# Hybrid decoder layer, its last two token chunks: output projections placed earlier, block sums of the activations made in the up stage, and the sums handed to VectorE

## The chip, the cores and the metric

One core of one Trainium2 chip runs the whole layer. The metric is the device time of one execution in microseconds (us); several executions are taken and their median is compared. Five engines work side by side, each in its own fixed order: TensorE (PE, its weight loads listed apart as PEld), VectorE (DVE), ScalarE (ACT), GpSimd (POOL), and SyncE (SP), which only issues DMAs. ACT issues DMAs as well.

## The reference, cut to what matters

One layer with three groups of heads (mLSTM, RWKV-7, differential attention) on 2048 tokens of width 1024, then an output projection, a feed-forward network (FFN) and a final norm:

```python
def _rms_norm(x, g, eps=NORM_EPS):
    xf = x.astype(jnp.float32)
    y = xf * lax.rsqrt(jnp.mean(jnp.square(xf), axis=-1, keepdims=True) + eps)
    return (y * g.astype(jnp.float32)).astype(x.dtype)
...
        mix = jnp.concatenate([y_m, y_r, y_a], axis=-1).astype(x.dtype)
        x = x + mix @ w_out[l]
        h = _rms_norm(x, norm2_g[l])
        x = x + jnp.square(jax.nn.relu(h @ w_ff_up[l])) @ w_ff_down[l]
    return _rms_norm(x, final_g)
```

The FFN is 1024 to 4096 and back. All of it is float32.

## The kernel before, in words

**Precision.** Every float32 product is three matmuls on a number cut in two (`split`, L174 and L175): ACT copies the high part (`whi`, `uh`, `hh`), VectorE or GpSimd subtracts it to get the low part (`wlo`, `ul`, `hl`), and TensorE adds high by high, high by low and low by high (L182 to L184 in `mm3`, L1219 to L1221 in `Wino.prod`). So each tile of weights costs one ACT and one DVE or POOL instruction before TensorE can use it.

**Stages.** Tokens are four chunks of 512. Projections, mLSTM, RWKV and attention run first; then `Tail` does, chunk by chunk, the output projection (`outproj`, 192 matmuls) and the FFN. Chunks 0 and 1 have a plain FFN (`ffn`), a loop of 16 steps `fb` with 48 up and 48 down matmuls each. Chunks 2 and 3 share one FFN by the Strassen-Winograd scheme (`Wino`): 7 block products instead of 8, at the price of sums of blocks. `first` norms chunk 2 and cuts its 8 tiles; `second` norms chunk 3, forms the sums t1 to t4 and cuts them; `up` makes the hidden layer and stores its activations to DRAM (`act`); `down` loads them again; `final` is the last norm. In all of them p counts the 7 products.

- `up`: 8 steps fb, 7 products p, two halves q of 12 matmuls each. The sums of weight blocks (`factors`, L1284 to L1290) are on VectorE, all low parts on GpSimd. The results are 4 blocks of 16 tiles, so 64 stores.
- `down`: 4 stages st, 7 products of 48 matmuls. VectorE makes sums of the loaded activations (L1368 to L1376, 16 tiles of 128x512 a stage), GpSimd makes the sums of weight blocks (L1284 to L1290, 8 tiles of 128x1024 a stage) and the low parts of the weights (28 a stage); VectorE makes the low parts of the activations (28 a stage). Each product has its own four PSUM banks, and VectorE adds them to an accumulator in SBUF (L1411). In the last stage 28 sums of accumulators on GpSimd (L1408, L1410) and 4 on VectorE (L1413) join the 7 products to the four blocks of the result.

**Placing.** `tile_hybrid_layer` runs chunk 1's FFN loop. It overlaps the attention of chunk 3, whose waits its matmuls fill. At `fb == 12` the attention's pools are closed (`actx.close()`), the pools of the next stage open in their place, and the output projection of chunk 2 starts; a step of it follows at fb 13 and 14; at fb 15 `Wino.first`, at fb 16 the output projection of chunk 3. Then comes `final(1, ...)` (chunk 1's norm and output) and `second`.

**What sets the order.** The order on each engine is fixed when the program is built: a scheduler places the instructions by their dependences and by priority (`high_priority`), with its own estimate of time. Pools bind it: a tile in a newly opened pool can't be written before the last reader of the closed pool. The norm's sum of squares (`nacc`, L155 to L168) has one buffer, so two norms can't overlap.

Of the kernel before, what the change touches and what calls it, by code (L numbers as in the profile page):

```python
# [20 lines left out]
P = 128  # L21
# [1179 lines left out]
class Wino:  # L1201
# [33 lines left out]
    def first(s, x2, hp):  # L1235

        nc = s.tc.nc
        with s.tc.high_priority():
            s.rms(x2)
            s.b11 = s.cut(x2[:4], [s.tl.hl(hp) for _ in range(4)], (nc.vector, nc.gpsimd))  # L1240
            s.b21 = s.cut(x2[4:], [s.tl.hl(hp) for _ in range(4)], (nc.vector, nc.gpsimd))

    def second(s, x2, x3, tp):
# [3 lines left out]
        with s.tc.high_priority():  # L1247
# [3 lines left out]
            for k in range(4):  # L1251
                G.tensor_tensor(b12[k], b22[k], b12[k], ALU.subtract)
                V.tensor_tensor(b11[k], b12[k], b11[k], ALU.add)
                t2 += s.cut(b11[k:k + 1], [tl.hl()], (V,))
            for k in range(4):
                t3 += s.cut(b12[k:k + 1], [tl.hl()], (G, V))
# [3 lines left out]
            for k in range(4):  # L1260
                G.tensor_tensor(b21[k], b21[k], b11[k], ALU.subtract)
                t4 += s.cut(b21[k:k + 1], [tl.hl(tp)], (V,))
# [3 lines left out]
    def factors(s, ring, bufs, a, eng):  # L1266

        nc = s.tc.nc

        def new():  # L1270
            return ring.tile([P, 1024], F32, name="wr", tag="wr", bufs=bufs)

        def ld(x):
            t = new()
            s.e.dq += 1
            load(nc, s.e.dq, t.rearrange("p (k c) -> p k c", k=x.shape[1]), x)
            return t
        a11 = ld(a[0])
        yield a11
        a12 = ld(a[1])  # L1280
        yield a12
        s3, a22 = ld(a[2]), ld(a[3])
        s2 = new()
        eng.tensor_tensor(s3, a11, s3, ALU.subtract)  # L1284
        eng.tensor_tensor(s2, a22, s3, ALU.subtract)
        yield s2
        yield s3
        s1, s4 = s3, s2
        eng.tensor_tensor(s1, s2, a11, ALU.add)
        eng.tensor_tensor(s4, a12, s2, ALU.subtract)  # L1290
        yield s1
        yield a22
        yield s4

    def unit(s, x, eng, shape):
# [3 lines left out]
        h3, l3 = [t.rearrange("p (k c) -> p k c", k=shape) if shape else t for t in (hi, lo)]  # L1299
# [3 lines left out]
    def up(s):  # L1303
        tc, nc, tl, e = s.tc, s.tc.nc, s.tl, s.e
        V, A = nc.vector, nc.scalar
        for fb in range(8):
            f = s.factors(s.wr, 6, [tl.wu[fb + 8 * m][:, 4 * k:4 * k + 4] for m in range(2) for k in range(2)], V)
            ps = [[None] * 3 for _ in range(2)]
            c1, u2, u3 = [[None] * 2 for _ in range(3)]

            def put(m, c, x, r):
                A.activation(r, x, AF.Relu)
                A.activation(r, r, AF.Square)
                nc.sync.dma_start(e.act[c][m], r)
            for p in range(7):
                b = (0, 0, 1, 1, 2, 1, 2)[p]
                new = p in (0, 2, 4)
                with tc.high_priority():
                    w = next(f).rearrange("p (k c) -> p k c", k=4)
                    w = [s.unit(w[:, :, q * P:(q + 1) * P], nc.gpsimd, 4) for q in range(2)]  # L1320
                for q in range(2):
                    if new:
                        ps[q][b] = s.bank(1 + b)
                    o = ps[q][b]
                    for k in range(4):
                        s.prod(o, w[q][0][:, k * P:(k + 1) * P], w[q][1][:, k * P:(k + 1) * P], s.ops[p][k], new and k == 0)
                    m = 2 * fb + q
                    with tc.high_priority():
                        if p == 0:
                            c1[q] = tl.slot(0)  # L1330
                            A.copy(c1[q], o)
                        elif p in (2, 3):
                            t = tl.slot(4)
                            V.tensor_tensor(t, o, c1[q], ALU.add)
                            (u2 if p == 2 else u3)[q] = t
                        else:
                            r = tl.slot(5)
                            if p == 1:
                                put(m, 0, o, r)
                            else:  # L1340
                                V.tensor_tensor(r, o, {4: u3, 5: c1, 6: u2}[p][q], ALU.add)
                                put(m + 16 * (p != 6), p != 5, r, r)

    def down(s, ap, ar, wr2):
        tc, nc, tl, e = s.tc, s.tc.nc, s.tl, s.e
        V, A, G = nc.vector, nc.scalar, nc.gpsimd
        grp = [0, 2, 3, 4, 5]
        acc = [[ap.tile([P, T], F32, name="acc", tag=f"a{p}{q}") if p < 6 else tl.slot(1) for q in range(4)] for p in range(7)]
        with tc.high_priority():
            for p, c, d in ((1, 0, 0), (5, 0, 4), (6, 1, 0)):  # L1350
# [3 lines left out]
        def features(st):  # L1354
            def ld(g, c, m):
                x = [tl.slot(g) for _ in range(4)]
                for k in range(4):
                    load(nc, k, x[k], e.act[c][m + k])
                return x
            g = grp  # L1360
            m = 4 * st
            b11 = ld(g[0], 0, m)
            yield b11
# [266 lines left out]
```

## Time and profile before

| | |
|---|---|
| median of 3 runs | 3099.58 us (3095.73 to 3113.41) |
| profiled execution | 3101.93 us, its span 3100.2 us |
| mean granted clock of TensorE | 0.964 of 2.4 GHz |
| busy in the span | PE 2893.9 us (93%), DVE 1911.5 (62%), POOL 1391.0 (45%), ACT 1299.1 (42%) |
| chunk 2's and 3's `up` | 2394 to 2693 us |
| their `down` | 2693 to 3070 us |
| after the last matmul of a product | 3069.66 to 3100.2 us |

Busy time is summed by engine; a busy PE is not a PE at its peak. The granted clock is given as a share of 2.4 GHz, so 0.50 is 1.2 GHz. In a window's row "x" counts instructions, and "released by" (the arrow) names the instruction that ended a wait. The 1.7 us between the span and the profiled time lie around the program.

### The profile page before, as it was taken

To read this page: it belongs to the slowest core of one execution; us is meant where nothing else is said; L and a number is where in the kernel's file an instruction comes from. 1 tells how busy PE (TensorE), PEld (TensorE's weight loads), DVE (VectorE), ACT (ScalarE), POOL (GpSimd) and SP (SyncE) were. 2 spreads that over 40 slices of the span, in tenths; PEclk is the share of its full clock that TensorE was granted. 3 is DMA by queue.
4 is the path that set the end of the run, shared out by engine and by line. 5 is a ranking of instruction groups with operands and counts; after the bars stand their busy time and mean duration, and the time that the engine had idled before them with its cause. 6 is when DMAs were issued, how large, how long until landed. Compare 5 with 4: busy or idle time off the path is not lost. (4 is left out here: it accounts for less than half of the span.)

```text
span 3100.2 us, 47371 instructions
## 1 busy us (share of the span) xinstructions
PE 2893.9 (93%) x16848; PEld 2365.7 (76%) x16848; DVE 1911.5 (62%) x4141; ACT 1299.1 (42%) x2577; POOL 1391.0 (45%) x1213
## 2 busy tenths in 40 slices
PE   8999999999999789999999999999984999899995
PEld 7877887778878677888888788887863888777773
DVE  6587879677872557555556855554347333379995
ACT  5333334232322445444544554444333555443342
POOL 4354444333332124333433333333445444487787
PEclk9999999999999899999999999999996999999997
DMA  8445333643634553443446334424441333533201
GB/s 304 127 148 193 85 93 81 222 113 88 202 108 126 152 144 110 127 110 88 120 116 177 112 96 114 111 82 138 144 149 43 121 109 110 207 119 102 87 24 54
DMA packets 303270, 383.97 MB, mean 124 GB/s; under 512 B 100885, under 2 KB 162614, under 8 KB 302010
## 3 DMA queue, kind: packets, MB, share of 16 engines
q1 hardware_dynamic: 218634, 264.93, 28.5%
q10 hardware_dynamic: 84400, 116.02, 12.6%
q8 instruction: 133, 2.18, 0.3%
q14 instruction: 103, 0.84, 0.1%
HBM read 285.66 MB, written 95.18 MB: 123 GB/s over the span
## 5 line engine op out<-in xcount | busy, mean ns | idle before, releaser
L175 POOL TENSOR_TENSOR wlo<-wraw,whi 128x512 fp32r<-128x512 f32 (+2 forms) x432 | 593.7, 1387 | 859.6 <-ACT whi L174 608.2
L175 POOL TENSOR_TENSOR wlo<-wr,whi 128x512 fp32r<-128x512 f32 x224 | 325.0, 1461 | 222.2 <-ACT whi L174 194.3
L174 ACT ACTIVATE whi<-wraw 128x512 fp32r<-128x512 f32 (+2 forms) x432 | 267.1, 625 | 325.8 <-PE pd L183 103.2
L183 PE MATMUL pd<-hl,whi 128*128 128x512 f32 x768 | 304.5, 397 | 6.9 <-DVE hl L175 6.9
L182 PE MATMUL pd<-hh,whi 128*128 128x512 f32 x768 | 302.3, 398 | 5.8 <-ACT hh L174 5.3
L184 PE MATMUL pd<-hh,wlo 128*128 128x512 f32 x768 | 301.2, 396 | 0.1
L1174 DVE TENSOR_TENSOR x<-py,x 128x512 f32<-128x512 f32 x256 | 174.8, 688 | 197.2 <-PE py L184 196.1
L1030 DVE TENSOR_SCALAR_CACHE_REDUCE E<-pS 128x512 f32<-128x512 f32 (+4 forms) x320 | 185.6, 607 | 147.9 <-PE pS L1027 88.5
L174 ACT ACTIVATE whi<-wr 128x512 fp32r<-128x512 f32 x224 | 139.7, 629 | 290.9 <-PE pd L1220 121.6
L182 PE MATMUL pd<-hhi,whi 128*128 128x512 f32 x544 | 222.9, 413 | 7.7 <-ACT hhi L279 6.7
L184 PE MATMUL pd<-hhi,wlo 128*128 128x512 f32 x544 | 222.2, 411 | 0.6 <-POOL wlo L175 0.6
L183 PE MATMUL pd<-hlo,whi 128*128 128x512 f32 x544 | 221.9, 410 | 0.7 <-DVE hlo L280 0.3
L182 PE MATMUL py<-ah,whi 128*128 128x512 f32 x512 | 207.0, 405 | 1.2 <-DVE x L1174 0.6
L183 PE MATMUL py<-al,whi 128*128 128x512 f32 x512 | 203.2, 397 | 0.4 <-DVE al L175 0.4
L184 PE MATMUL py<-ah,wlo 128*128 128x512 f32 x512 | 201.6, 397 | 0.0
L1037 ACT ACTIVATE E<-E,nm 128x128 f32<-128x128 f32 (+15 forms) x128 | 153.7, 1201 | 91.1 <-DVE nm L1033 73.9
L182 PE MATMUL pd<-whi,hhi 128*128 128x256 f32 (+1 forms) x640 | 187.1, 293 | 1.2 <-ACT gates L372 0.9
L183 PE MATMUL pd<-wlo,hhi 128*128 128x256 f32 (+1 forms) x640 | 186.9, 292 | 0.0
L175 DVE TENSOR_TENSOR ul<-x,uh 128x512 fp32r<-128x512 f32 x112 | 155.8, 1404 | 49.1 <-ACT uh L174 49.1
L184 PE MATMUL pd<-whi,hlo 128*128 128x256 f32 (+1 forms) x640 | 185.7, 290 | 0.0
L183 PEld LDWEIGHTS pd<-hl,whi 128*128 128x128 f32 x768 | 145.7, 190 | 37.6 <-DVE hl L175 7.3
L182 PEld LDWEIGHTS pd<-hh,whi 128*128 128x128 f32 x768 | 145.3, 190 | 37.2 <-issue 5.6
(447 smaller groups left out, 7302.9 us busy)
## 6 DMA issues: line engine op xcount, KB each, us to landing
wraw<-in_wu ACTq DMA_DIRECT2D x64, 256.0 KB, 3.1
wraw<-in_wu SPq DMA_DIRECT2D x64, 256.0 KB, 3.2
wraw<-in_wd ACTq DMA_DIRECT2D x64, 256.0 KB, 3.3
wraw<-in_wd SPq DMA_DIRECT2D x64, 256.0 KB, 3.0
act<-x SPq DMA_DIRECT2D x64, 256.0 KB, 2.0
wraw<-in_wi ACTq DMA_DIRECT2D x48, 256.0 KB, 3.5
wraw<-in_wi SPq DMA_DIRECT2D x48, 256.0 KB, 3.6
feat<-hhi SPq DMA_DIRECT2D x4, 2048.0 KB, 9.7
```

The lines of the kernel that those rows point to most:

```text
L174: nc.scalar.activation(hi, src, AF.Copy)
L175: lo_eng.tensor_tensor(lo, src, hi.bitcast(F32), ALU.subtract)
L182: nc.tensor.matmul(out, sh, mh, start=(i == 0), stop=False)
L183: nc.tensor.matmul(out, sh, ml, start=False, stop=False)
L184: nc.tensor.matmul(out, sl, mh, start=False, stop=(i == n - 1))
L1030: V.tensor_scalar(E[:, k0:k0 + w], s_[:, :w], 0.125, None, ALU.mult, ALU.max, accum_out=mb[:, j:j + 1])
L1037: A.activation(E[:, :n], E[:, :n], AF.Exp, bias=nm, accum_out=l)
L1174: nc.vector.tensor_tensor(x2[d], ps, x2[d], ALU.add)
```

## The change

1. The attention's pools are closed at `fb == 8` instead of 12. The output projection of chunk 2 runs at fb 8 to 12, `Wino.first` at fb 12 instead of 15, the output projection of chunk 3 at fb 12 to 15 instead of after the loop.
2. `up` takes its products in another order and half q after half (12 matmuls a product). Low parts are on GpSimd for 3 of 7 products and on VectorE for 4; the sums of weight blocks are made per half on VectorE. The sums of activation blocks are made here, four a half on VectorE, and all 7 blocks are stored: 112 stores instead of 64. Three PSUM banks are each used for two or three products of a half, and what the first left is read before the next adds to it.
3. `down` loads 7 finished blocks (112 loads) and makes no sums of them. The sums of weight blocks move to VectorE; the low parts of weights go half to GpSimd, half to VectorE. PSUM banks of one product are kept and added to by a later one (`NEW`, `BANK`), so 24 sums of accumulators are left in the last stage, 20 on VectorE and 4 on GpSimd. (Of `final(2, ...)` 2 tiles instead of 8 are on GpSimd.)

```diff
+    NEW = (0, 1, 4)
+    BANK = (0, 1, 0, 1, 2, 1, 2)
...
-                G.tensor_tensor(b12[k], b22[k], b12[k], ALU.subtract)
+                V.tensor_tensor(b12[k], b22[k], b12[k], ALU.subtract)
...
-        s.ops = [s.b11, s.b21, t2, t3, t1, t4, c22]
+        s.ops = [s.b11, t2, s.b21, t3, t1, t4, c22]
...
+            for q in range(2):
+                f = s.factors([t.rearrange("p (k c) -> p k c", k=4)[:, :, q * P:(q + 1) * P] for t in w])
...
+                        h, l = s.unit(next(f), nc.gpsimd if p in (0, 3, 5) else V, 4)
+                    if p in s.NEW:
+                        ps[s.BANK[p]] = s.bank(1 + s.BANK[p])
...
+                    V.tensor_tensor(b12, b22, b12, ALU.subtract)
+                    put(3, b12)
+                    V.tensor_tensor(b11, b12, b11, ALU.add)
+                    put(1, b11)
+                    V.tensor_tensor(t1, b22, b11, ALU.subtract)
+                    put(4, t1)
+                    V.tensor_tensor(b21, b21, b11, ALU.subtract)
+                    put(5, b21)
...
-                        w = s.unit(ws[k // 2][:, k % 2 * T:k % 2 * T + T], G, 0)
+                        w = s.unit(ws[k // 2][:, k % 2 * T:k % 2 * T + T], V if k % 2 else G)
...
-                            for i in {1: (0,), 2: (0,), 3: (2,), 5: (3,), 6: (2, 4)}.get(p, ()):
-                                G.tensor_tensor(a, a, acc[i][q], ALU.add)
...
+                            for y, z, eng in {0: ((x22[q], a[0], G), (a[5], a[0], V)), 1: ((a[1], a[0], V), (a[6], a[1], V)),
+                                              3: ((x22[q], a[3], V),), 4: ((x22[q], a[4], V),)}.get(p, ()):
+                                eng.tensor_tensor(y, y, z, ALU.add)
...
-        if fb == 12:
+        if fb == 8:
             actx.close()
...
+        if 8 < fb < 12:
+            next(op)
+        if fb == 12:
+            list(op)
+            wn = Wino(tl, wr, pq)
+            wn.first(x2)
+            op = tl.outproj(3, tl.load(3, hp2), x3, (4, 5), pq[1], e.x2d[1])
```

**In the program's order, TensorE, end of chunk 3's attention.** L1051 are transposes and L1056 products of the last head, L1068 the transposes of its output; `pd<-hh,whi` and `py<-ah,whi` are matmuls of chunk 1's FFN. Before, they stand around the transposes:

```order
L182 MATMUL py<-ah,whi 128x512
L183 MATMUL py<-al,whi 128x512
L184 MATMUL py<-ah,wlo 128x512
L182 MATMUL py<-ah,whi 128x512
L1068 MATMUL pT<-ident,osb 128x128 x2
L183 MATMUL py<-al,whi 128x512
L1068 MATMUL pT<-ident,osb 128x128 x2
L184 MATMUL py<-ah,wlo 128x512
L183 MATMUL pd<-hl,whi 128x512
L184 MATMUL pd<-hh,wlo 128x512
```

In the changed kernel the same place reads as follows; here the first `pd` after the transposes is the output projection of chunk 2.

```order
L1056 MATMUL pO<-Vt,PT 128x128 x4
L1051 MATMUL pT<-ident,E 128x128 x4
L1056 MATMUL pO<-Vt,PT 128x128 x4
L1051 MATMUL pT<-ident,E 128x128 x4
L1056 MATMUL pO<-Vt,PT 128x128 x4
L1051 MATMUL pT<-ident,E 128x128 x4
L1056 MATMUL pO<-Vt,PT 128x128 x4
L1068 MATMUL pT<-ident,osb 128x128 x4
L182 MATMUL pd<-hh,whi 128x512 x2
L183 MATMUL pd<-hl,whi 128x512
L184 MATMUL pd<-hh,wlo 128x512
```

FFN matmuls no longer stand between the last head's steps, and the output projection follows it directly.

**VectorE, a product of `down`.** L175 makes low parts, L1411 adds PSUM to an accumulator. Before, the sums of activations (L1373, L1376) stand between them:

```order
L1411 TENSOR_TENSOR acc<-pd,acc 128x512 x2
L175 TENSOR_TENSOR ul<-x,uh 128x512
L1373 TENSOR_TENSOR x<-x 128x512
L1376 TENSOR_TENSOR x<-x 128x512
L175 TENSOR_TENSOR ul<-x,uh 128x512
L1373 TENSOR_TENSOR x<-x 128x512
L1376 TENSOR_TENSOR x<-x 128x512
```

In the changed kernel the low parts of weights (`wlo`) and the sums of weight blocks (128x1024) stand there:

```order
L1411 TENSOR_TENSOR acc<-pd,acc 128x512 x2
L175 TENSOR_TENSOR wlo<-wr,whi 128x512
L175 TENSOR_TENSOR ul<-x,uh 128x512 x2
L1286 TENSOR_TENSOR wr<-wr 128x1024
L175 TENSOR_TENSOR wlo<-wr,whi 128x512
L175 TENSOR_TENSOR ul<-x,uh 128x512 x2
L175 TENSOR_TENSOR wlo<-wr,whi 128x512
L175 TENSOR_TENSOR ul<-x,uh 128x512
L1287 TENSOR_TENSOR wr<-wr 128x1024
```

VectorE has lost the sums of activations and gained two `wlo` a product and the wide sums.

**GpSimd, `down`.** Before, wide sums (L1284 to L1290) stand among the low parts of weights:

```order
L1289 TENSOR_TENSOR wr<-wr 128x1024
L175 TENSOR_TENSOR wlo<-wr,whi 128x512
L1284 TENSOR_TENSOR wr<-wr 128x1024
L1290 TENSOR_TENSOR wr<-wr 128x1024
L175 TENSOR_TENSOR wlo<-wr,whi 128x512 x5
L1285 TENSOR_TENSOR wr<-wr 128x1024
L1284 TENSOR_TENSOR wr<-wr 128x1024
L175 TENSOR_TENSOR wlo<-wr,whi 128x512 x5
```

In the changed kernel this is all that GpSimd has from the cuts of `second` to the end:

```order
L175 TENSOR_TENSOR hl<-x,hh 128x512 x5
L175 TENSOR_TENSOR x<-x 128x512
L175 TENSOR_TENSOR wlo<-wr,whi 128x512 x92
L1416 TENSOR_TENSOR x<-x,acc 128x512 x4
L175 TENSOR_TENSOR wlo<-wr,whi 128x512 x9
L134 TENSOR_TENSOR nsm<-nsm,nhalf 128x4
L1192 TENSOR_TENSOR acc<-acc,nacc 128x512 x2
L134 TENSOR_TENSOR nsm<-nsm,nhalf 128x4
L1192 TENSOR_TENSOR x<-x,nacc 128x512 x3
```

One kind of work is left there, with half the number of tiles per product of `down`.

## Rows read from the trace of the kernel before

**Rows 1.** Page, part 1: busy time and share of the span.

```profile
PE 2893.9 (93%) x16848; PEld 2365.7 (76%) x16848; DVE 1911.5 (62%) x4141; ACT 1299.1 (42%) x2577; POOL 1391.0 (45%) x1213
```

**Rows 2.** Windows: length, busy time (instructions) per engine, granted clock, DMA share, GB/s.

```profile
1025.00:1125.00 100.00, 72.89 (x340) 54.51 (x339) 59.97 (x232) 48.28 (x136) 17.14 (x14) 0.81 0.58 162
2035.00:2146.00 111.00, 111.00 (x580) 94.02 (x579) 50.66 (x97) 47.17 (x84) 40.60 (x30) 1.00 0.26 80
2146.00:2249.00 103.00, 97.67 (x412) 78.48 (x411) 38.66 (x47) 40.67 (x70) 47.12 (x36) 0.97 0.53 166
2249.00:2331.00 82.00, 71.95 (x292) 57.28 (x291) 40.70 (x54) 29.42 (x50) 39.04 (x29) 0.92 0.46 138
2331.00:2394.00 63.00, 21.85 (x70) 14.54 (x69) 47.44 (x51) 18.25 (x33) 34.72 (x22) 0.64 0.14 50
2394.00:2693.00 299.00, 299.00 (x1296) 245.22 (x1297) 104.77 (x124) 151.22 (x252) 149.54 (x109) 0.99 0.34 118
2400.00:2675.00 275.00, 275.00 (x1203) 225.68 (x1202) 91.21 (x106) 140.45 (x233) 137.47 (x101) 1.00 0.33 113
2693.00:3070.00 377.00, 336.95 (x1355) 261.70 (x1353) 311.58 (x282) 146.94 (x261) 298.53 (x172) 0.95 0.28 88
2712.00:3070.00 358.00, 327.09 (x1322) 254.16 (x1320) 305.97 (x273) 139.51 (x248) 294.48 (x169) 0.96 0.24 73
```

**Rows 3.** Waits of PE, 2100 to 3101: total, times, longest.

```profile
PE nps L162 <- DVE nacc L159: 30.8, 4, 15.2
PE pd L1220 <- DVE ul L175: 18.9, 12, 4.0
PE pd L1219 <- ACT whi L174: 9.1, 1, 9.1
PE pd L1221 <- POOL wlo L175: 5.7, 3, 3.8
```

**Rows 4.** Groups by form in 2712 to 3070: busy, mean ns, idle before.

```profile
L175 POOL TENSOR_TENSOR wlo<-wr,whi 128x512 fp32r<-128x512 f32 x107 | 165.1, 1558 | 51.3 <-ACT whi L174 46.9 <-PE pd L1220 4.4
L175 DVE TENSOR_TENSOR ul<-x,uh 128x512 fp32r<-128x512 f32 x105 | 149.0, 1431 | 41.0 <-ACT uh L174 41.0
L1411 DVE TENSOR_TENSOR acc<-pd,acc 128x512 f32<-128x512 f32 x60 | 39.5, 679 | 5.6 <-PE pd L1221 4.3 <-POOL acc L1408 1.2
L1376 DVE TENSOR_TENSOR x<-x 128x512 f32<-128x512 f32 x16 | 30.8, 1923 | 0.4
L1290 POOL TENSOR_TENSOR wr<-wr 128x1024 f32<-128x1024 f32 x8 | 22.6, 2828 | 0.0
```

**Rows 5.** Timeline: store of the last head, then what waits (ACT, PE).

```profile
2147.33 0.33 SPq L1071 DMA_DIRECT2D mixT<-ot  x1
2154.44 0.63 ACT L174 ACTIVATE hh<-traw 128x512 fp32r<-128x512 f32 x1 [6.08 <-DMA mixT<-ot]
2155.17 1.19 PE L182 MATMUL pd<-hh,whi 128*128 128x512 f32 x2 [4.93 <-ACT hh L174]
```

**Rows 6.** Timeline: one half block of attention (DVE, ACT, DVE).

```profile
2099.56 0.69 DVE L1030 TENSOR_SCALAR_CACHE_REDUCE E<-pS 128x512 f32<-128x512 f32 x1 [0.21 <-PE pS L1027]
2101.10 2.01 ACT L1037 ACTIVATE E<-E,nm 128x2048 f32<-128x2048 f32 x1 [1.41 <-DVE nm L1033]
2104.43 2.34 DVE L1045 SCALAR_TENSOR_TENSOR E<-E,rat 128x2048 f32<-128x2048 f32 x1
2110.97 0.35 DVE L1057 TENSOR_SCALAR osb<-pO,orl 128x128 f32<-128x128 f32 x1 [0.44 <-PE pO L1056]
```

**Rows 7.** Timeline: chunk 1's final norm, then `down`'s first weights.

```profile
2337.24 1.26 POOL L175 TENSOR_TENSOR wlo<-wr,whi 128x512 fp32r<-128x512 f32 x1 [1.17 <-ACT whi L174]
2338.53 1.23 DVE L1289 TENSOR_TENSOR wr<-wr 128x1024 f32<-128x1024 f32 x1 [0.88 <-POOL wlo L175]
2695.32 0.69 DVE L175 TENSOR_TENSOR ul<-x,uh 128x512 fp32r<-128x512 f32 x1 [1.29 <-ACT uh L174]
2700.35 0.58 SPq L42 DMA_DIRECT2D wr<-in_wd  x1
2707.92 0.79 PE L1219 MATMUL pd<-uh,whi 128*128 128x512 f32 x1 [9.14 <-ACT whi L174]
```

**Rows 8.** Timeline: the end.

```profile
3066.65 9.86 POOL L1192 TENSOR_TENSOR acc<-acc,nacc 128x512 f32<-128x512 f32 x8 [4.79 <-ACT nacc L168]
3076.54 0.63 ACT L155 ACTIVATE nacc<-x 128x512 f32<-128x512 f32 x1 [9.96 <-POOL acc L1192]
```

More of the change, by code (lines that the diff above doesn't have):

```diff
@@ L1233, in cut, with first @@
         return pairs
-    def first(s, x2, hp):
+    def first(s, x2):
         nc = s.tc.nc
@@ L1239, in first, with second @@
             s.rms(x2)
-            s.b11 = s.cut(x2[:4], [s.tl.hl(hp) for _ in range(4)], (nc.vector, nc.gpsimd))
-            s.b21 = s.cut(x2[4:], [s.tl.hl(hp) for _ in range(4)], (nc.vector, nc.gpsimd))
-    def second(s, x2, x3, tp):
+            s.b11 = s.cut(x2[:4], [s.tl.hl() for _ in range(4)], (nc.vector, nc.gpsimd))
+            s.b21 = s.cut(x2[4:], [s.tl.hl() for _ in range(4)], (nc.vector, nc.gpsimd))
+    def second(s, x2, x3, hp, tp):
         nc, tl = s.tc.nc, s.tl
@@ L1306, in up @@
         for fb in range(8):
[L1307 to L1324, printed above, removed]
+            with tc.high_priority():
+                w = s.blocks(s.wr, 6, [tl.wu[fb + 8 * m][:, 4 * k:4 * k + 4] for m in range(2) for k in range(2)])
@@ L1379, in down, with four @@
+        def four(src, again=True):
+            g = grp.pop(0)
+            if again:
+                grp.append(g)
+            x = [tl.slot(g) for _ in range(4)]
+            for k in range(4):
+                load(nc, k, x[k], src[k])
+            return x
         for st in range(4):
             last = st == 3
-            x = features(st)
-            f = [s.factors(r, n, [tl.wd[2 * st + i + 8 * k][:, :, T * m:T * m + T] for m in range(2) for k in range(2)], G)
-                 for i, (r, n) in enumerate(((s.wr, 6), (wr2, 5)))]
+            with tc.high_priority():
+                f = [s.factors(s.blocks(r, b, [tl.wd[2 * st + i + 8 * k][:, :, T * m:T * m + T] for m in range(2) for k in range(2)]))
+                     for i, (r, b) in enumerate(((s.wr, 6), (wr2, 5)))]
+            ps = {}
@@ L1396, in down @@
                     if last and p == 0:
-                        x22 = [tl.slot(grp[4]) for _ in range(4)]
-                        for q in range(4):
-                            load(nc, q, x22[q], e.x2d[1][4 + q])
+                        x22 = four(e.x2d[1][4:], False)
                     for q in range(4):
-                        a = acc[p][q]
-                        if st == 0 and p in (0, 2, 3, 4):
-                            A.copy(a, ps[q])
+                        a = [t[q] for t in acc]
@@ L1441, in tile_hybrid_layer @@
     e.av = [scr(f"av{h}", [HALF, 512]) for h in range(2)]
[L1442 removed]
+    e.act = [[scr(f"act{c}_{m}", [P, T]) for m in range(FF // P // 2)] for c in range(7)]
     e.x2d = [[scr(f"x2d{c}_{d}", [P, T]) for d in range(KT)] for c in range(2)]
@@ L1547, in tile_hybrid_layer @@
             list(op)
-            wn = Wino(tl, wr, pq)
-            wn.first(x2, hp2)
-            m3 = tl.load(3)
-        if fb == 16:
-            for _ in tl.outproj(3, m3, x3, (4, 5), None, e.x2d[1]):
-                pass
     tl.final(1, x1, (2, 5))
```

144 lines of the change are left out of this document (68 added, 76 removed).

## Prediction

> **What bounds the kernel now.** First the busy shares: TensorE works 93% of the span [rows 1]. Unless its matmuls become fewer, and they don't, a change can only win back the other 7% and stretches at the lower clock. So the second view is the windows, to find where TensorE is not full. While attention and chunk 1's FFN run together (2035 to 2146) and in `up` it is full; 1203 matmuls in 275 us are 0.2286 us each, which I take as its pace [rows 2]. It loses time in three places. From 2146 to 2331 the 704 matmul records would need 161 us and take 185: 24 lost. From 2331 to 2394, around chunk 1's final norm and the norm of chunk 3, it is busy 21.85 of 63 us, at a mean clock of 0.64. And `down`, 2693 to 3070, holds 4 x 7 x 48 = 1344 matmuls, which need 307 us and take 377: 70 lost, the largest sum, and the one this change is about. Third, what PE waits for [rows 3]: the norms' sums (L162, 30.8 us), then low parts from VectorE (18.9) and GpSimd (5.7), and once 9.1 us for the first weights of `down`. Last, the two engines that make these low parts. In 2712 to 3070 VectorE is busy 306 and GpSimd 294 of 358 us [rows 2], so each looks as if it had room. The groups say otherwise: a 128x512 low part takes VectorE 1431 ns and GpSimd 1558 on the mean, a sum of activations (L1376) VectorE 1923 [rows 4], but 0.69 and 1.26 us where the other is idle [rows 7]; VectorE's additions out of PSUM, in the same stretch, keep to 679 ns [rows 4]. So the two slow each other down only where both inputs of VectorE lie in SBUF. Counted at the undisturbed times, GpSimd has 107 low parts and 28 sums x 1.26 and 30 wide sums x 2.52 (twice 1.26, an estimate), 246 us; VectorE has 105 low parts and 56 sums x 0.69, 111 us. Together 357 of 358 us: taken as one server the pair is full, and TensorE waits for it.
>
> The Trainium skill, page SBUF — State Buffer, section Who interferes with whom, has a rule for that: a VectorE instruction with two inputs in SBUF and a GpSimd instruction that reads SBUF exclude each other for their whole length, and one with a single SBUF input doesn't take part. The 1431, 1558 and 679 ns agree with it. By it, work that only changes sides stays in the same queue, so that of the moved sums only the shorter time on VectorE counts. With neither engine waiting for the other there would be no full server before (246 and 111 of 358 us), and the change would win in `down` only the 3 us of its entry, for some 3114 us in all.
>
> **The change part by part**, each against the profiled execution, 3101.9 us (the median lies 2.3 us lower).
>
> 1. `down`. Removed: 16 sums of activations a stage, and 28 + 4 sums of accumulators in the last one, of which 4 on GpSimd and 20 on VectorE remain. Moved from GpSimd to VectorE: 32 wide sums, at 1.23 us [rows 7] instead of 2.8 [rows 4], and half of the weights' low parts. After it GpSimd has 56 low parts and 4 sums, 60 x 1.26 = 76 us. VectorE has 112 + 56 low parts and 20 sums x 0.69 = 130, and 32 x 1.23 = 39, so 169 with both inputs in SBUF, and 96 additions out of PSUM x 0.68 = 65. The pair needs 245 instead of 357 us where TensorE needs 307. VectorE alone has 234; if every GpSimd instruction held it up, 310. So TensorE sets the pace again but for four things: the last stage, where p = 0 has 6 GpSimd instructions (7.6 us), 10 low parts and sums of VectorE (6.9) and a wide sum or so (1.4), 15.9 against the 11.0 of 48 matmuls, and p = 1 has 13.6: with the norm of chunk 2 some 10 us lost; the entry, 6 us (below); and in-order waits of single products, 8. Loss 24 instead of 70: **46 won**. Bounds: 30, if all of GpSimd's time holds VectorE up and the single waits cost 20; 54, if only the entry and the last stage cost. I take 46 because the pair's load falls by a third and the waits of PE here are of that pair's making [rows 3]. What was hidden stays so: 48 more loads of 256 KB run on DMA engines whose share here is 0.24 [rows 2].
>    The entry: TensorE waits 9.14 us, since the weights for k = 2 and 3 are only issued on SP at 2700.35, behind stores [rows 7]. After it, ACT issues them behind its last square; I price it at 6 (4 to 9).
>
> 2. The output projections. What the order shows decides here: with the pools closed at fb 8, FFN matmuls of later steps no longer stand between the steps of chunk 3's last head. Before, they filled its waits wholly: 111.00 of 111 us [rows 2]. Three and a half blocks of that head are left bare. A block occupies VectorE with 8 maxima of 0.69 or less, the scaling of 2.34 and small ones, some 8.5 us [rows 6]; 3.5 x 8.5 = 30; the last one ends with the exponential (2.0), the scaling (2.3) and 4.2 from there to the last L1057 [rows 6], and some 2 for the head's norm: 41 us, of which the matmuls fill about 25 (an estimate from their number). 16 lost. Then the output projection needs the stored head: from the issue of the store at 2147.33 to the cut at 2154.44 are 7.1 us [rows 5], and with copy and cut 9; before, FFN matmuls covered all but 4.93 of it. Its later tiles arrive at the pace of VectorE's cuts (4), and the clock has to rise again (3, an estimate). 32 lost against 24 before, and in exchange chunk 2's norm and chunk 3's projection run among FFN matmuls, which I price at nothing lost: the FFN of four steps covers them, and without this cover they cost the 20 that lie in those 24 besides the store. **8 lost** (5 won, if only store and cut cost; 25 lost, by A below).
>
> 3. The gap of 63 us between the FFN and `up` stays: `final(1, ...)` still precedes chunk 3's norm, by the one buffer. Off VectorE's path in it go the wide sums between L164 and L144, 2 x 1.23 [rows 7] and one more; on it come 4 subtractions from GpSimd (2.8), and TensorE has 12 matmuls less to fill with (2.7). **0** (8 either way).
>
> 4. `up`. A half is 84 matmuls, 19.2 us. In it VectorE has 4 low parts, 4 sums of weights, 4 of activations and 5 evictions, 17 x 0.69 = 11.7, GpSimd 3 x 1.26 = 3.8: 15.5 of 19.2 even in turn. ACT keeps its work (151 of 299 us [rows 2]). New is the hand-over of banks: four times a half a product adds to a bank that was filled two products earlier, with one product, 12 x 0.2286 = 2.74 us, to read it. An eviction of 0.69 leaves 2 us of room, more than one foreign instruction. **5 lost** over 64 hand-overs (0 to 15). 48 more stores stand on SP; its loads stand behind them, one step ahead.
>
> 5. The end. `final(3)` waits for GpSimd's 8 multiplications, 9.86 us to 3076.5, 6.9 after the last matmul [rows 8]. VectorE takes 6 of them, but behind its last additions: 9 after. **2 lost** (1 to 3).
>
> Sum: 46 - 8 - 0 - 5 - 2 = 31 us won, 3071 from the profiled execution; beside the median I put **3070**.
>
> **Rivals.**
> A. The bare head costs more. In 1025 to 1125, attention with little beside it, TensorE is busy 72.89 of 100 us at a clock of 0.81 [rows 2], so 59 us of work. By that the head's 25 and the projection's first 17 us of work take 71, 29 lost instead of 16, and with half clock on the wait for the store some 49 in all: 25 lost in step 2 and 46 - 25 - 5 - 2 = 14 won, **3088**: no change. For it: the windows in which TensorE idles have the lower clocks, 0.81 here and 0.64 at 2331 [rows 2]. Against it: that stretch also waits for loads at its start.
> B. Slower: the hand-over of banks in `up`. If an eviction stands behind two foreign instructions at the disturbed 1.43 to 1.75 us, it ends 3.7 us after the product or later, 1 us past the 2.74; from 2.74 on every microsecond is TensorE's. 64 x 1.0 = 64 lost in step 4 instead of 5, and 46 - 8 - 64 - 2 = 28 lost: **3130**. For it: VectorE's queue is in order, and sums that wait for ACT's squares stand in it. Against it: GpSimd has 3 instructions in 19.2 us.
> C. VectorE inherits the limit in `down`: if its instructions with two SBUF inputs keep the 1.43 us [rows 4], 188 of them and 32 wide ones at twice the 1.23 are 348 us, and with 65 out of PSUM over 400; with half of that increase, 169 + 90 + 65 = 324, and 45 for entry, last stage and single waits `down` takes 369: 8 won instead of 46, 7 lost in all, **3109**, no change. Against it: the increase is GpSimd's time, which falls from 294 to about 76.
>
> **How the numbers follow.** Forecast 0.66, spread from 3040 (steps 1 to 4 at their better ends, not all) to 3084; A 0.14, C 0.06, B 0.14. The measurement tells about 0.5%, 15 us. Faster 0.66, same 0.20, slower 0.14. The range takes in A and C and leaves out B and a little below: 3040 to 3110.
>
> **What would show it.** Step 1: `down` lasts about 331 us from its first matmul, VectorE's low parts near 0.8 us, GpSimd busy under 110 us in it, waits for `ul` gone. Step 2: windows of TensorE under 20 of 25 us around 2070 to 2130 that weren't there, and the 2146 to 2331 losses gone. Step 4: waits of PE in `up` named after evictions would speak for B. It is wrong if `down` stays over 350 us, or the bare head loses over 40.

## The result, and the profile after

The changed kernel takes 3089.26 us (median of 18 runs, 3078.06 to 3100.93) against 3104.89 (18 runs, 3095.73 to 3118.53) of the kernel before on the same chip: ratio 0.9949, 95% interval 0.9936 to 0.9962, that is 15.8 us less (12 to 20). The forecast was 3070, some 31 us won. The time lies in the stated range, the sign is right, and the size is half of what was forecast, at the edge of the 0.5% that the prediction could tell apart.

The profiled execution of the changed kernel took 3098.3 us, with a span of 3096.6. The two traces can't be laid over each other from the start: the same attention matmul (L1026, the 20th from the last) begins at 2025.2 us before and at 2035.7 after, though the same 12794 matmul records stand ahead of it, all but 8 of them in the same places. In the traces of the experiments this point lies between 2025 and 2049 us, with no relation to what was changed. So only what follows it is compared: 1075.0 us before, 1060.9 after, 14.1 less, which agrees with the medians.

Page, part 1, of the changed kernel, to be read beside [rows 1]; GpSimd has lost 321 us, VectorE gained 36:

```profile
PE 2898.9 (94%) x16848; PEld 2376.1 (77%) x16848; DVE 1947.5 (63%) x4355; ACT 1297.8 (42%) x2571; POOL 1069.5 (35%) x1023
```

Windows of the changed kernel, columns as in [rows 2]: the last head; the wait for its store; the rest of the FFN with both projections; the gap around the norms; `up`; the entry to `down` (two rows); the rest of it; the end.

```profile
2036.00:2098.00 62.00, 48.26 (x265) 39.53 (x263) 25.64 (x70) 23.03 (x40) 8.44 (x6) 0.82 0.12 36
2098.00:2111.00 13.00, 1.20 (x4) 0.70 (x4) 3.35 (x6) 2.01 (x4) 0.00 (x0) 0.50 0.66 222
2111.00:2363.00 252.00, 248.66 (x1060) 201.08 (x1058) 105.22 (x140) 98.96 (x168) 120.87 (x89) 0.98 0.42 130
2363.00:2420.00 57.00, 20.97 (x62) 13.35 (x61) 43.25 (x62) 20.52 (x36) 19.55 (x12) 0.61 0.10 37
2420.00:2714.00 294.00, 293.08 (x1279) 240.12 (x1279) 189.31 (x264) 145.38 (x244) 61.80 (x46) 1.00 0.43 150
2714.00:2750.00 36.00, 14.61 (x52) 11.13 (x51) 9.99 (x16) 8.91 (x16) 0.50 (x1) 0.75 0.97 351
2750.00:3062.00 312.00, 312.00 (x1327) 250.84 (x1326) 251.26 (x314) 135.73 (x240) 89.56 (x60) 0.99 0.37 121
3062.00:3096.00 34.00, 5.58 (x15) 2.71 (x13) 20.92 (x28) 7.92 (x13) 8.53 (x6) 0.56 0.33 123
```

The reader is to see a new hole at 2036 to 2111, a longer one at 2714 to 2750, and a `down` that is full from 2750 to its end, where before it was busy 327 of 358 us [rows 2]. In the entry the DMA engines are busy for 0.97 of the time. Before, the share was 0.28 over the whole of `down` [rows 2], but its entry was as full as now, only shorter:

```profile
2693.00:2712.00 19.00, 9.86 (x35) 7.53 (x34) 5.61 (x9) 7.43 (x13) 4.05 (x4) 0.77 1.02 364
```

What PE waits for in the changed kernel, 2030 to 3100:

```profile
PE nps L162 <- DVE nacc L159: 30.2, 4, 13.6
PE pd L1223 <- ACT whi L174: 15.8, 1, 15.8
PE pd L182 <- ACT hh L174: 11.8, 1, 11.8
PE pd L1223 <- ACT hh L174: 11.4, 1, 11.4
PE nps L145 <- DVE traw L144: 9.8, 4, 2.7
PE pO L1056 <- ACT PT L1053: 9.3, 10, 2.3
PE pd L1223 <- ACT uh L174: 5.5, 1, 5.5
PE py L1223 <- ACT x L1336: 2.3, 1, 2.3
```

The 18.9 us for `ul` and 5.7 for `wlo` of [rows 3] are gone. In their place stand single long waits: 11.8 for the first cut tile of chunk 2's projection, 5.5 and 15.8 at the entry to `down` (before, one of 9.1 [rows 3]). One wait only, of 2.3 us, is put down to an eviction in `up`, ACT's copy (L1336).

The groups in `down`, 2791 to 3062, beside [rows 4]: `ul` has fallen from 1431 to 948 ns, while GpSimd's `wlo` is nearly as slow as it was (1506 against 1558); VectorE's new `wlo` takes 750, its additions out of PSUM 679 as before.

```profile
L175 DVE TENSOR_TENSOR ul<-x,uh 128x512 fp32r<-128x512 f32 x94 | 88.8, 948 | 13.7 <-ACT uh L174 13.7
L175 POOL TENSOR_TENSOR wlo<-wr,whi 128x512 fp32r<-128x512 f32 x46 | 69.3, 1506 | 182.5 <-ACT whi L174 171.6 <-PE pd L1225 6.7 <-DVE x L1416 4.2
L1411 DVE TENSOR_TENSOR acc<-pd,acc 128x512 f32<-128x512 f32 x57 | 37.4, 679 | 8.4 <-PE pd L1225 8.4
L175 DVE TENSOR_TENSOR wlo<-wr,whi 128x512 fp32r<-128x512 f32 x46 | 34.5, 750 | 19.5 <-ACT whi L174 19.5
```

To see where the time went I add up, for each stretch of each trace, the time from the start of one matmul to the start of the next, less 0.2273 us for 512 columns and in proportion for fewer. The rest is TensorE's lost time (idle, or at half clock). The few matmuls of the norms (L145, L162) have prices of their own; in strict proportion the head would be 0.6 higher and the middle 1.8 in every row, and the body 0.4, or 1.8 where it is that of before. "Head" runs from the L1026 named above to the last L1068, "middle" on to the last FFN matmul, "gap" to 15 us after the last norm before `up`, "entry" from up's end over the first 192 matmuls of `down`, "body" over its other 1152. Us:

```
                      head  middle  gap    up   entry  body
before                10.2   25.8  47.4   4.7   13.2   55.5
after                 33.7   24.0  44.1   2.6   28.2    8.5
old placing (e1)      10.2   25.6  41.8   4.4   29.2    8.4
new placing only (e2) 31.4   20.6  48.5   4.5   13.9   54.0
late residuals (e3)   33.7   23.5  44.1   2.6   21.9    8.4
GpSimd sums (e4)      32.8   21.4  44.1   2.6   25.0   17.0
closed at 10 (e5)     26.1   22.3  44.6   2.6   26.6    8.5
halves swapped (e6)   33.7   23.6  44.2   3.9   21.9    8.5
16 more sums (e8)     32.8   21.1  44.1   2.6   21.2   19.2
both of these (e9)    33.7   23.4  44.0   2.7   29.7   53.1
weights ahead (e10)   33.7   23.4  44.0   4.1   20.1    8.4
closed at 12 (e12)    10.2   18.3  44.1   2.6   25.9    8.4
all together (e11)    10.2   18.4  44.2   3.7   14.1    8.5
no residuals (e13)    33.7   23.3  44.0   2.7   18.0    8.4
```

The 10.2 in the head of "before" is the price of many narrow matmuls, not idle time (TensorE is busy 111.00 of 111 us there [rows 2]). Where `up` and `down` are built alike (after, e1, e5, e12), the body agrees within 0.1 us and the entry lies between 25.9 and 29.2.

### The profile page after: what moved, and what is told of

It reads as the page before. It is cut to its first block, busy times and chain, and to the rows that moved or that the text cites. A ratio compares the mean times of both kernels' runs of the same rounds, so it can differ in the third digit from the quotient of the medians.

```text
span 3096.6 us, 47520 instructions
## 1 busy us (share of the span) xinstructions
PE 2898.9 (94%) x16848; PEld 2376.1 (77%) x16848; DVE 1947.5 (63%) x4355; ACT 1297.8 (42%) x2571; POOL 1069.5 (35%) x1023
## 5 line engine op out<-in xcount | busy, mean ns | idle before, releaser
L175 POOL TENSOR_TENSOR wlo<-wraw,whi 128x512 fp32r<-128x512 f32 (+2 forms) x432 | 591.6, 1381 | 825.4 <-ACT whi L174 545.4
L175 POOL TENSOR_TENSOR wlo<-wr,whi 128x512 fp32r<-128x512 f32 x104 | 148.6, 1430 | 486.6 <-ACT whi L174 401.4
L1056 PEld LDWEIGHTS pO<-Vt,PT 128*128 128x128 f32 x1088 | 151.9, 202 | 36.1 <-ACT PT L1053 25.8
L1056 PE MATMUL pO<-Vt,PT 128*128 128x128 f32 x1088 | 160.4, 290 | 18.8 <-ACT PT L1053 18.8
```

The costliest lines, as they stand in the source:

```text
L175: lo_eng.tensor_tensor(lo, src, hi.bitcast(F32), ALU.subtract)
L1056: PE.matmul(o[:, 0:P], pt[:, b * P:(b + 1) * P], vt[:, kb], start=(kb == 0), stop=(kb == i))
```

## The experiments

**Theory.** The relief of `down` came as forecast, by the load of the pair VectorE and GpSimd. Half of it was given back in two places: the last head with the wait for its store, which lost their cover, and the entry to `down`. **Rivals.** The placing pays, and the missing part was lost in `up` or `down`; or the gain in `down` has another source, the removed activation sums alone or the engine shift alone. The ratios below are to runs of the kernel before on the same chip; the changed kernel's own is 0.9949 (0.9936 to 0.9962).

### e1 and e2: each half of the change alone

e1 has the new `up` and `down` and the old placing:

```diff
-        if fb == 8:
+        if fb == 12:
             actx.close()
...
-        if 8 < fb < 12:
-            next(op)
-        if fb == 12:
+        if 12 < fb < 15:
+            next(op)
+        if fb == 15:
             list(op)
             wn = Wino(tl, wr, pq)
-            wn.first(x2)
-            op = tl.outproj(3, tl.load(3, hp2), x3, (4, 5), pq[1], e.x2d[1])
+            wn.first(x2, hp2)
+            m3 = tl.load(3)
+        if fb == 16:
+            for _ in tl.outproj(3, m3, x3, (4, 5), None, e.x2d[1]):
+                pass
```

> The changed up and down stages with the output projections of chunks 2 and 3 where they were (pools closed at fb 12, first at 15, chunk 3's projection after the loop). Theory: the bare last head and the wait for its store cost 22 us more than they gave back, so about 3070 us, 18 to 22 less than the changed kernel's 3089, and the last head stands among FFN matmuls again (PE full there). Rival: the new placing pays for itself and the missing gain was lost in up and down; then this kernel is at 3089 or slower.

e2 is the reverse, in the kernel before:

> The new placing alone, with the up and down stages of before. Theory: about 20 us slower than before, 3125, with PE idle some 12 us ahead of chunk 2's projection and at half clock in the last head. Rival: the placing pays, 3105 or less.

Measured: e1 3077.26 us, ratio 0.9894 (0.9875 to 0.9913), 17 us below the changed kernel; e2 3128.4, ratio 1.0062 (1.0042 to 1.0081), 19 us slower than before. The two ratios multiply to 0.9955: the ratio of the whole change, 0.9949, is that within the intervals, so that no interaction of the halves shows. The new placing costs 17 to 19 us; the rival falls. Windows of e1, head and middle:

```profile
2041.00:2160.00 119.00, 119.00 (x619) 100.61 (x618) 54.64 (x108) 53.01 (x91) 44.46 (x33) 1.00 0.30 86
2160.00:2346.00 186.00, 170.21 (x709) 136.15 (x708) 79.72 (x107) 70.33 (x119) 84.44 (x62) 0.95 0.49 153
```

TensorE is full again in the head. In the changed kernel, at the end of it (ACT, SP and PE in one stretch), the output of the last head is copied at 2099.44 and stored, and TensorE has nothing to do until it has been loaded and cut:

```profile
2099.44 0.58 ACT L1070 COPY ot<-pT 128x512 f32<-128x512 f32 x1 [4.52 <-issue]
2100.05 0.74 SPq L1071 DMA_DIRECT2D mixT<-ot  x1
2109.58 1.67 ACT L174 ACTIVATE hh<-traw 128x512 fp32r<-128x512 f32 x3 [9.55 <-DMA mixT<-ot]
2110.30 1.19 PE L182 MATMUL pd<-hh,whi 128*128 128x512 f32 x2 [11.80 <-ACT hh L174]
```

Before, 4.93 us of this were bare [rows 5].

### e5 and e12: where the pools are closed

e5 closes them at fb 10, with the projections at 10 to 13 and 13 to 15. e12 closes them at 12, but keeps both projections amid the FFN:

```diff
-        if fb == 8:
+        if fb == 12:
             actx.close()
...
-        if 8 < fb < 12:
-            next(op)
-        if fb == 12:
+        if fb == 13:
+            next(op), next(op)
+        if fb == 14:
             list(op)
...
-        if 12 < fb < 15:
-            next(op)
         if fb == 15:
+            next(op), next(op)
+        if fb == 16:
             list(op)
```

> The changed kernel with the attention's pools closed at fb 10 instead of 8, chunk 2's projection at 10 to 13, the first norm at 13 and chunk 3's projection at 13 to 15. Theory: two more FFN steps stand among the last head's steps (each some 22 us of matmuls for a head that is bare for some 60 us); the head loses 10 to 15 us instead of 34, the wait for its store (12 us) stays: 3066 to 3074, 15 to 20 below the changed kernel. Rival: what is missing is the work moved ahead of the norms, so that with less of it left for them the middle (2098 to 2363) loses more and the sum stays within 5 us of the changed kernel.

> The changed kernel with the pools closed at fb 12, but both projections still amid the FFN: chunk 2's at 12 to 14, the first norm at 14, chunk 3's at 14 to 16. Theory: the head stands wholly among FFN matmuls (loss 10 instead of 34), the store's wait falls to about 5 us, and the middle keeps some of the filling: 3060 to 3070, at or a little below the kernel with the old placing. Rival: with 4 steps of FFN left for two projections and a norm the middle loses 30 us or more; then it stays at 3080 or above.

Measured: e5 3083.12 us, ratio 0.9925 (0.9900 to 0.9951), 7 us less than the changed kernel, half of what was expected; e12 3070.46, ratio 0.9876 (0.9853 to 0.9898), 23 us less. In e5 two more FFN steps stand in the head, 99 us long instead of 62, but it is bare at its end all the same, and the wait for the store is unchanged (windows of e5: head, then that wait):

```profile
2044.00:2143.00 99.00, 90.32 (x461) 75.95 (x459) 41.11 (x93) 39.50 (x68) 30.63 (x22) 0.91 0.26 75
2143.00:2156.00 13.00, 1.27 (x4) 0.79 (x4) 3.59 (x6) 2.25 (x4) 0.00 (x0) 0.50 0.67 222
```

The loss falls from 33.7 to 26.1 only: what the fillers cover is the first part, and the dearest part is the last one, the transposes and products that follow the last scaling (L1045); from there to the last L1068 are 19 us in both traces, of which 16 are lost in both. With the pools closed at 12 the head is covered and the wait for the store is 5.7 us, and the two projections amid four FFN steps lose 18.3 us in the middle instead of 25.6 (e1). So the idea of step 2 seems sound, worth some 7 us by the traces and 6 by the ratios, whose intervals overlap; only the place for it was too early.

### e4, e8 and e9: what relieved `down`

e4 puts all of the weights' low parts and sums in `down` back on GpSimd (the sums by handing GpSimd to `factors`, which is not shown here); e8 adds 16 sums a stage on VectorE, as many as there were for the activations; e9 has both.

```diff
-                        w = s.unit(ws[k // 2][:, k % 2 * T:k % 2 * T + T], V if k % 2 else G)
+                        w = s.unit(ws[k // 2][:, k % 2 * T:k % 2 * T + T], G)
...
+                    for y in ((1, 3), (1, 3), (1, 3), (1, 2, 3), (1, 2, 3), (1, 3), (1, 3))[p]:
+                        d = tl.raw()
+                        V.tensor_tensor(d, x[y], x[y - 1], ALU.subtract)
```

> The changed kernel, with all low parts and all block sums of the weights in down back on GpSimd; the activations' sums stay in up and the sums of accumulators as in the change. Theory (one server for both engines): GpSimd 112 x 1.26 + 32 x 2.52 + 5 = 227 us, VectorE 132 x 0.69 = 91, together 318 where the matmuls need 307: down loses 15 to 30 us more than in the changed kernel, 3104 to 3119. Rival: what relieved down was only the removal of the activations' sums, and the shift between the engines is worth nothing: 3089.

> The changed kernel with 16 more sums of 128x512 a stage on VectorE in down (both inputs in SBUF, into a scratch tile that nothing reads), as many as the kernel before has there for the activations. One-server theory: the pair's load rises from 245 to 289 us where the matmuls need 307, so little changes: 0 to 8 us slower than the changed kernel. Rival: removing those sums is what relieved down, whatever the rest; then 25 to 40 us of the loss come back.

> As the kernel with all weight low parts and weight sums of down on GpSimd, and the 16 more sums a stage on VectorE as well. One-server theory: 318 + 44 = 362 us of load for 307 us of matmuls; down loses some 40 us more than without the sums, 45 to 55 more than the changed kernel's: 3130 to 3145. Rival (each engine by itself): GpSimd 227 and VectorE 135 + 65 us both fit in 307, so the sums cost less than 10 us.

Measured: e4 3101.71 us, ratio 0.9971 (0.9958 to 0.9984); e8 3097.51, ratio 0.9962 (0.9945 to 0.9978); e9 3137.83, ratio 1.0092 (1.0067 to 1.0118). The last 1152 matmuls of `down`, in windows of e4, e8 and e9, to which the same stretch of e2 (the `down` of before) is added as the last row:

```profile
2785.00:3064.00 279.00, 273.41 (x1160) 219.10 (x1159) 208.08 (x211) 112.68 (x199) 210.53 (x123) 0.99 0.38 111
2773.00:3055.00 282.00, 274.28 (x1164) 217.18 (x1162) 250.34 (x331) 110.56 (x200) 77.04 (x51) 1.00 0.37 113
2784.00:3100.00 316.00, 285.03 (x1163) 221.74 (x1161) 260.63 (x261) 112.04 (x203) 210.76 (x121) 0.97 0.33 100
2791.00:3109.00 318.00, 289.44 (x1163) 223.64 (x1162) 275.99 (x252) 123.30 (x218) 259.96 (x151) 0.96 0.24 73
```

In the changed kernel this stretch takes 271 us. Beside it stand the loads of the pair, counted at undisturbed times as in the prediction, for the whole of `down`: 245 us (changed), 289 (e8), 318 (e4), 362 (e9), 357 (before), where the matmuls need 307. Above 307 the excess is 11, 55 and 50 us; the stretch is 0.88 of `down`, so 10, 48 and 44 are to be expected in it, and 8, 45 and 47 are found. e4 loses less than the 15 to 30 expected, e9 is at the lower end of its 45 to 55. e8's load stays under 307 and costs 11 us in its stretch, though by the ratios only 4, within the intervals; its waits are nine short ones for `ul`, 7.6 us together. So near the limit the sum is off by as much as e4's whole excess. There is a reason that isn't the pair's load: the added sums stand in VectorE's order where their inputs have not all been loaded, and VectorE is idle 13.4 us for that in e8 and 23.9 in e9 (group of the sums in the same windows), where before L1376 waited 0.4 [rows 4]:

```profile
L1406 DVE TENSOR_TENSOR traw<-x 128x512 f32<-128x512 f32 x44 | 36.7, 834 | 13.5 <-DMA x<-act 13.4
L1406 DVE TENSOR_TENSOR traw<-x 128x512 f32<-128x512 f32 x43 | 66.4, 1545 | 24.0 <-DMA x<-act 23.9
```

How much of e8's 11 and e9's 45 us is this was not tried; in e4 and before, such waits are 1.6 and 2.7 us. Taken by itself each engine has room in all five (in e9 GpSimd is busy 211 and VectorE 261 of 316 us), and yet the sums alone cost 11 us, the shift back alone 8, and both 45. Causes that don't touch would have added up to 19; a limit that both engines share gives the rest. So the one-server reading stands as an account of the large excesses, not as an exact rule, and neither the removed sums nor the shift alone explains the gain.

### e3, e6, e10 and e13: the entry to `down`

e3 moves the loads of residuals, four each, behind the products p = 1, 4 and 5 in the program (not behind the first, as its expectation has it); e13 leaves them out.

```diff
-        with tc.high_priority():
-            for p, c, d in ((2, 0, 0), (5, 0, 4), (6, 1, 0)):
-                for q in range(4):
-                    load(nc, q, acc[p][q], e.x2d[c][d + q])
...
+                if st == 0 and p in (1, 4, 5):
+                    c, d = {1: (0, 0), 4: (0, 4), 5: (1, 0)}[p]
+                    for q in range(4):
+                        load(nc, q, acc[{1: 2}.get(p, p + 1)][q], e.x2d[c][d + q])
```

> The changed kernel, with the 12 loads of residuals (256 KB each, 3 MB) into down's accumulators placed behind its first product in program order instead of ahead of the stage. Theory: the 16 us wait ahead of product 0's third quarter is DMA bandwidth (DMA share over 0.9, some 400 GB/s there), and 3 MB less in front of the second ring's weights takes up to 7 us off it: 3082 to 3086. Rival: the wait is set by the release of the up stage's tiles, after which the second ring's loads may start, and by their own landing; then nothing changes, 3089.

> The changed kernel without the 12 loads of residuals into down's accumulators (3 MB): the first stage's products are copied into them instead, so 12 of the 16 residual tiles are missing from the result, and 12 additions of VectorE become copies of ACT. If DMA bandwidth sets the entry's waits, 3 MB at some 400 GB/s are 7.5 us less, entry loss 18 to 22 and 6 to 9 us below the changed kernel, as with the later loads. If the release of up's tiles sets it, the wait for the first weights of the second ring stays at 14 to 16 us and the time within 3 us.

e6 places the first halves of two products ahead of their second halves; e10 adds weights loaded ahead for the second half of product 0.

```diff
+            if st == 0:
+                begin(0), step(0, 0), step(0, 1), begin(1), step(1, 0), step(1, 1)
...
+                    ahead = [s.tl.w.wp.tile([P, T], F32, name="wraw", tag="wraw", bufs=3) for _ in range(2)]
+                    for k in range(2):
+                        load(nc, k, ahead[k], tl.wd[1][:, k, 0:T])
```

> The changed kernel, with the first halves (k = 0, 1: weights of the first ring) of products 0 and 1 of down's first stage both placed ahead of their second halves, whose weights come in the ring that is only free once up has ended. Theory: TensorE waits 5.9 and 16.2 us at the entry, for the landing of those weights; 24 more matmuls (5.5 us at full clock, up to 11 at half) cover part of it: 5 to 10 us less than the changed kernel. Rival: VectorE or the loads of the activations are as late as the weights, and the wait only moves: 3089.

> The changed kernel with the halves of down's first two products swapped as before, and the second half of product 0's weights loaded a second time, during up, into the two free raw tiles of the earlier FFN. Traffic is 0.5 MB more, but 72 matmuls (16 us) instead of 24 stand ahead of the first weights that must wait for up's tiles to be released. Theory (release of the ring, then landing): the 10.7 to 16 us wait shrinks to a few us or goes, entry loss from 22-28 to 10-14 us, 8 to 14 us below the changed kernel. Rival (DMA bandwidth, some 16 MB in the 52 us of the entry): the activations come as late, the wait moves to them and the time stays within 4 us.

Measured: e3 3087.56 us, ratio 0.9924 (0.9906 to 0.9942); e13 3087.72, ratio 0.9912 (0.9887 to 0.9936); e6 3090.5, ratio 0.9947 (0.9929 to 0.9965); e10 3086.41, ratio 0.9934 (0.9911 to 0.9957). TensorE's waits at the entry, first of the changed kernel, then of e13:

```profile
2720.05 0.79 PE L1223 MATMUL pd<-uh,whi 128*128 128x512 f32 x1 [5.54 <-ACT uh L174]
2749.42 0.80 PE L1223 MATMUL pd<-uh,whi 128*128 128x512 f32 x1 [15.85 <-ACT whi L174]
```

```profile
2723.83 0.80 PE L1223 MATMUL pd<-uh,whi 128*128 128x512 f32 x1 [5.80 <-ACT uh L174]
2743.39 0.79 PE L1223 MATMUL pd<-uh,whi 128*128 128x512 f32 x1 [6.42 <-ACT whi L174]
```

With 3 MB less traffic the second wait falls from 15.85 to 6.42 us and the time by 11 (the first wait, for the activations of product 0, stays). That looks like bandwidth: at the 351 GB/s of the entry's window 3 MB take 8.5 us. ACT's rows say otherwise. These are the load of the weights that are cut next, what ACT issues after it, and the cut; first in the changed kernel, then in e13:

```profile
2735.60 0.56 ACTq L42 DMA_DIRECT2D wr<-in_wd  x1
2741.96 0.33 ACTq L42 DMA_DIRECT2D x<-act  x1
2747.10 1.59 ACTq L42 DMA_DIRECT2D x<-x2d  x2
2748.74 1.67 ACT L174 ACTIVATE whi<-wr 128x512 fp32r<-128x512 f32 x3 [11.91 <-DMA act<-traw]
```

```profile
2732.84 0.56 ACTq L42 DMA_DIRECT2D wr<-in_wd  x1
2742.33 0.33 ACTq L42 DMA_DIRECT2D x<-act  x1
2742.70 2.19 ACT L174 ACTIVATE whi<-wr 128x512 fp32r<-128x512 f32 x4 [5.07 <-DVE wr L1286]
```

In the changed kernel the load lands 6.3 us after its issue, at 2741.9. Before, it took as long, from 2700.35 [rows 7] to 2706.6, and the cut followed 0.6 us behind it:

```profile
2707.24 2.19 ACT L174 ACTIVATE whi<-wr 128x512 fp32r<-128x512 f32 x4 [6.28 <-DMA wr<-in_wd]
```

Now the cut comes 6.9 us after the landing. ACT's order is fixed, and ahead of the cut stand issues of other loads, the last two of residuals (`x<-x2d`, at 2747.10 and 2748.37); by the semaphores in the trace each starts 0.02 us after an earlier transfer has landed. These 6.9 us instead of 0.6 are nearly all of the 6.7 by which this wait has grown since before. In e13 the load takes longer to land, 8.1 us (VectorE's L1286 starts on it at 2741.05), but it is issued 4.1 us ahead of TensorE's stop instead of 2.0 behind it, and the cut follows 1.8 us after. So the 9.4 us come from the earlier issue (6.2) and from an ACT that is free for the cut (5.1), less the slower landing (1.8). Nor is it the release of up's tiles that holds the load in the changed kernel: its issue at 2735.60 follows the landing of a residual load (`acc<-x2d`) at 2735.57; in e13 and e3 it follows a matmul.

Moving the loads (e3) gives 8 us by the ratios, with a wait of 10.8 in the trace; six of the twelve are still issued before this wait ends, three of them on ACT, one after the other ahead of the cut. In e9, which wasn't meant for the entry, another order came out: seven residual loads are issued by then, none of `x<-x2d`, and the wait is 6.34 us, as short as without any. Swapping the halves (e6) gives nothing by the ratios, where 5 to 10 were expected; TensorE then waits 10.7 us for the cut of the same weights, which had landed at 2728.2, some 9 us before its end. With weights ahead (e10) it still waits 13.5, at another product, for a sum of weight blocks; its 5 us, less than the 8 to 14 expected, are within the intervals. No run changed the order of ACT's issues alone, with the same loads; that would part the order from the traffic.

### e11: all together

Placing of e12, later loads, swapped halves and weights ahead.

> All together: pools closed at fb 12 with both projections amid the FFN, the residuals' loads later, the halves of the first two products of down swapped and product 0's second weights loaded ahead. If the parts add: 20 to 28 us from the placing and 8 to 14 from the entry below the changed kernel, 3050 to 3062, faster than both kernels. If the entry is DMA bandwidth: as the kernel with the placing alone.

Measured: 3051.23 us (3045.88 to 3061.07), ratio 0.9826 (0.9799 to 0.9853), 54 us less than before and 38 less than the changed kernel: faster than both. Windows of it: head, middle, entry, body; then its two waits at the entry:

```profile
2025.00:2144.00 119.00, 119.00 (x618) 100.56 (x617) 54.79 (x110) 52.88 (x91) 44.65 (x33) 1.00 0.30 86
2144.00:2323.00 179.00, 167.79 (x710) 132.65 (x709) 79.98 (x106) 69.15 (x119) 86.40 (x62) 0.98 0.54 162
2678.00:2739.00 61.00, 52.04 (x208) 41.11 (x207) 39.60 (x47) 28.75 (x53) 13.16 (x9) 0.92 0.91 319
2739.00:3010.00 271.00, 271.00 (x1162) 217.85 (x1160) 218.94 (x281) 115.23 (x203) 75.25 (x51) 1.00 0.36 111
```

```profile
PE pd L1223 <- ACT whi L174: 6.8, 1, 6.8
PE pd L1223 <- ACT uh L174: 2.2, 1, 2.2
```

The entry's parts together take it from 25.9 (e12) to 14.1 us; later loads (6.3) and swapped halves with weights ahead (8.1) would by themselves add up to 14.4. The rival, that bandwidth leaves the time at e12's, falls: e11 moves 0.5 MB more than e12 and is 15 us faster by the ratios.

## Why the prediction was wrong in size

**Step 1, the body: right** (47 won, where 46 were forecast for body and entry together). VectorE and GpSimd as one server: the loss falls from 55.5 to 8.5 us, and e4 and e9 follow the same sum; e8 loses more than it gives. GpSimd is busy 89.56 us in 2750 to 3062, under the 110 named; `ul` takes 0.95 us, not 0.8. The last stage, priced at 10, costs less, since the whole body loses 8.5. From its first matmul `down` lasts 342 us (2720.05 to 3062), where 331 were forecast; the 11 more lie in the entry.

**Step 1, the entry: failed.** The price was "6 (4 to 9)" for one wait of TensorE, from a single row, the issue of the weights on SP [rows 7]; ACT was to issue them now, behind its last square. The sentence "What was hidden stays so: 48 more loads of 256 KB run on DMA engines whose share here is 0.24" took its share from 2712 on, behind the entry; in the entry it was 1.02 already before. 28.2 us are lost there instead of 13.2: 15 lost where 3 won were forecast. In place of one wait of 9.1 us there are two, a new one of 5.5 for the first activations (ACT's `uh` at 2719.37 has waited 7.4 us for `x<-act`) and 15.9 for the cut of the weights. The load of these lands as fast as before; what the prediction had wrong is the path: the cut stands in ACT's order behind issues of other loads, and each of these is held until an earlier transfer lands, 6.9 us. That the loads and stores which the change added cause this was not tried by itself: from 2700 to 2752 us 16.43 MB are moved, from 2680 to 2715 before 12.06, and e13 took away loads that stood there before the change too.

**Step 2, the placing: mechanism right, size wrong.** Forecast 32 lost instead of 24; found, for head and middle, 57.7 instead of 36.0, so 22 lost instead of 8; e1 and e2 give 17 to 19. Two terms failed. The head loses 23.5 more than before, not 16: its last part runs at the lower clock (mean 0.53 of 2.4 GHz in 2075 to 2100), where the sum had taken its 25 us of matmuls at full clock; that this is the whole difference was not tried. And the price of nothing for the norm and chunk 3's projection among FFN matmuls was wrong: besides the 12 us at the store the middle still loses 12 of its 24. Rival A had 25 lost in this step, and a time of 3088. Its mechanism for this term is right, but that it hit the time is luck: it kept the full 46 of step 1, and had 5 lost in `up`, where 2.1 were won.

**Steps 3 to 5: right, or off by little.** The gap wins 3.3 us (forecast 0, 8 either way). `up` loses nothing by the hand-over of banks, 2.6 instead of 4.7 us (forecast 5 lost, 0 to 15), so rival B falls. The end, from the last product's matmul to the end of the span, grows from 30.9 to 34.4 us, 3.5 lost (forecast 2, 1 to 3).

**Rival C falls:** VectorE's low parts come down to 0.75 and 0.95 us, and its sums of accumulators (L1416) take 0.77 to 1.01.

The sum by the traces: 47 won in the body, 15 lost at the entry, 21.7 lost in head and middle, 3.3 and 2.1 won, 3.5 lost: 12 of the 14.1 by which the tails differ.

## What to carry to other kernels

Two engines whose instructions slow each other down can be counted as one server: add up their undisturbed times for these instructions and set the sum against the bound engine's time; here that told the excess of the three overloaded variants of one stage to within 3 us, and busy shares of each engine by itself told nothing. It is no fine measure: a fourth variant, at 0.94 of full load, lost 11 us that the sum doesn't give. When work is moved earlier, price what it uncovers by the length of the chain left bare, at the clock that falls with it (0.53 of 2.4 GHz here), and include the way through DRAM that ends it. A stage's entry needs its own look: an average share over the stage hides a burst at its first products (0.24 against 1.02), and where an engine issues loads itself, its next work stands behind every issue that is held until an earlier transfer lands.

## What the runs showed of the hardware

- GpSimd's low part of 128x512 takes 1506 ns in the changed kernel, beside a VectorE that is busy 0.81 of the time, against 1558 before, although the pair's load fell by a third; it is VectorE's side that got faster (`ul` from 1431 to 948). VectorE's additions out of PSUM took 676 to 683 ns in all variants of `down`, with GpSimd busy 77 to 294 us in it.
- Over the same matmuls, nearly all in the same order, the first two thirds of the span differ by up to 24 us from trace to trace, while the body of `down` repeats within 0.1 us where it is built alike.
- A load of 512 KB took 6.3 us from issue to landing in the entry to `down` of both kernels, at DMA shares of 0.97 and 1.02, and 8.1 in e13; ACT could use it 6.9, 0.6 and 1.8 us later, by what stood ahead in its order.
